# Splitting float32 weights in the DMA instead of on VectorE and GpSimd, in a two-layer encoder trunk

## The chip, the cores and the metric

The kernel runs on one core of a Trainium2 chip. The metric is the device time of one execution in microseconds; lower is better. TensorE (PE in the profile) multiplies, VectorE (DVE), ScalarE (ACT) and GpSimd (POOL) work on tiles in the on-chip memory, SyncE (SP) issues DMAs. Every engine takes its own instructions in a fixed order, and waits where an operand or a buffer is not ready.

## What is computed

```python
for l in range(DEPTH):                                                  # 2 layers
    x = x + 0.5 * swiglu(rms_norm(x, ffn1_norm[l]), ffn1_w_in[l], ffn1_w_out[l])
    x = x + hybrid_mixer(rms_norm(x, mix_norm[l]), mix_w_in[l], ...)    # conv | stick-breaking | retention
    x = x + 0.5 * swiglu(rms_norm(x, ffn2_norm[l]), ffn2_w_in[l], ffn2_w_out[l])
return rms_norm(x, final_norm)

def swiglu(h, w_in, w_out):
    gate, up = jnp.split(h @ w_in, 2, axis=-1)
    return (jax.nn.silu(gate) * up) @ w_out
```

x has 512 rows of 1024 float32 numbers. The hidden size of the half steps is 2816, 22 blocks of 128. The mixer projects to 24 blocks of 128 columns, runs a causal convolution of 31 taps on 256 channels, eight heads of stick-breaking attention and four of retention, and projects back.

## The kernel before

x lies transposed: eight tiles of 128 features by 512 tokens. All products use float32r operands, each float32 operand being split into two of them, a high part `hi` (the number rounded to float32r) and a low part `lo` (the rest). A product of a weight block with a block of x takes three matmuls of 512 columns: `hi` by x's high part, `hi` by x's low part, `lo` by x's high part (`product`). Each of them streams 512 columns.

A weight unit is what one accumulator needs: 128 output features by up to eight blocks of 128 input features, [128, 8, 128] float32, 512 KB, each partition's share being contiguous in HBM. Units are

- `f1_in`, `f2_in`: 44 a half step (gate and up for each of 22 blocks), eight blocks each, accumulators `pg` and `pu` (`pf` for the first two);
- `f1_out`, `f2_out`: eight output tiles for each of three parts of the hidden size, of 8, 8 and 6 blocks, accumulator `po`;
- `m_in`: 24 a mixer, accumulators `pf` (the first four, in `conv_in`) and `pj`;
- `m_out`: eight output tiles in two halves of four blocks, accumulator `mo` (`out_first`, `out_last`).

For each unit `load` issues a DMA from SP into `w_raw`; `split_unit` then lets ScalarE cast it into `w_hi` (`split_of`), and VectorE subtract to get `w_lo`. In the middle of the mixer (`weight`, called by `project` and `out_first`) GpSimd subtracts. The two units at the very start are loaded and split in halves of four blocks, with the cast on VectorE. The pool `w` has three buffers each of `w_raw`, `w_hi` and `w_lo`.

The half step (`ffn`) runs over the 22 blocks in three parts; within a part first gate and up for each block, with `g`, `s`, `u` (scale, silu, product) and the split of the result into `hh` and `hl`, then the eight output tiles, each added to x through `t`: on GpSimd in the first two parts, on VectorE in the last. The norm's sum of squares uses ScalarE (`sq`) and GpSimd, its inverse root is a power on GpSimd (`rt`), and its spread over the partitions a matmul (`bc`, copied to `rstd`).

The mixer is made of threads whose instructions are interleaved when the program is built, by `weave`, after estimates in `Times`: an instruction of GpSimd is booked as 0.13 us plus 0.00286 us an element of a partition, a DMA of SP as 2.5 us. VectorE takes the taps of the convolution's first half (`yc`), ScalarE and GpSimd most of those of the second.

The order on every engine and queue is fixed before the run by the framework's scheduler, from its own estimate of when each operand and buffer is ready; it need not be the order of the program's lines. Semaphores are placed by it too. Every recorded instruction goes through `TimedEngine.run`, so the profile gives line 92 for all.

Of the kernel before, what the change touches and what calls it, by code (L numbers as in the profile page):

```python
# [4 lines left out]
F32 = mybir.dt.float32  # L5
# [6 lines left out]
P = 128  # L12
# [15 lines left out]

# of the mixer's order of work, in us: the slack before a product's operands are taken to be there, the time from one
# engine to another, how far behind the tensor engine the others may be, and the time between taps of the convolution  # L30
MARGIN, SIGNAL, BEHIND, PACE = 0.6, 0.2, 4.0, 2.3
# engine -> (time of an instruction, time per element)
COST = {"vector": (0.08, 0.00137), "scalar": (0.16, 0.00101), "gpsimd": (0.13, 0.00286)}
STEP = 4  # parts of a product between which other work may come
SHARED_TAPS = 24  # taps that ScalarE and GpSimd take for the second half of the channels


class Times:
    """Estimates, in us, of when instructions end, for the order in which to give them out."""

# [29 lines left out]
class Timed:  # L70
    """The machine, with a note of each instruction's times."""

# [24 lines left out]
class Kernel:  # L97
    def __init__(self, tc, io, out):
        self.tc, self.nc, self.io, self.out = tc, Timed(tc.nc), io, out

# [1 line left out]
    def split_of(self, src, hi, lo, engine=None, early=False):  # L102
# [6 lines left out]

    def load(self, src, n, step=KT):  # L110
        raw = self.wpool.tile([P, KT, P], F32, name="w_raw", tag="w_raw")
        for k in range(0, n, step):
            e = min(k + step, n)
            self.nc.sync.dma_start(raw[:, k:e, :], src[:, k:e, :])
        return raw

    def split_unit(self, raw, n, engine=None, step=KT):
        hi = self.wpool.tile([P, KT, P], F32R, name="w_hi", tag="w_hi")
        lo = self.wpool.tile([P, KT, P], F32R, name="w_lo", tag="w_lo")
        for k in range(0, n, step):  # L120
            e = min(k + step, n)
            self.split_of(raw[:, k:e, :], hi[:, k:e, :], lo[:, k:e, :], engine, step < KT)
        return hi, lo

    def unit(self, src, n, engine=None):
        return self.split_unit(self.load(src, n), n, engine)

    def product(self, acc, w, rhs_hi, rhs_lo, order, first=True, last=True):
        """acc[M, S] (+)= sum over order's (k of w, k of rhs) of w_k.T @ rhs_k, both operands in two parts."""
        hi, lo = w  # L130
        mm = self.nc.tensor.matmul
        for i, (a, b) in enumerate(order):
            mm(acc, hi[:, a, :], rhs_hi[b], start=first and i == 0, stop=False)
            mm(acc, hi[:, a, :], rhs_lo[b], start=False, stop=False)
            mm(acc, lo[:, a, :], rhs_hi[b], start=False, stop=last and i == len(order) - 1)
# [4 lines left out]
    def products(self, units, rhs_hi, rhs_lo):  # L140
        """Products of several weight units with rhs, whose parts get ready one by one."""
        accs = [self.bank("pf") for _ in units]
        for k in range(KT):
            for acc, w in zip(accs, units):
                self.product(acc, w, rhs_hi, rhs_lo, [(k, k)], k == 0, k == KT - 1)
        return accs

# [1 line left out]
    def new_norm(self):  # L149
        self.acc = []  # L150

    def norm_add(self, d, last=False, engine=None):
        """Adds x[d]'s squares to the running sum over d."""
        nc = self.nc
        sq = self.small.tile([P, S], F32, name="sq", tag="sq" if d else "sq_acc")
        nc.scalar.activation(sq, self.x[d], ACT.Square)
        if d and not (last and d == KT - 1):
            (engine or nc.gpsimd).tensor_tensor(out=self.acc[0], in0=self.acc[0], in1=sq, op=ALU.add)
        else:
            self.acc.append(sq)  # L160
# [11 lines left out]
    def diagonals(self, r):  # L172
        """[token, TT] -> [P, S], each token's value on the diagonal of its tile."""
        dg = self.small.tile([P, TT, P], F32, name="dg", tag="dg")
# [22 lines left out]
    def x_ready(self, d, g, engine=None):  # L197
        """x[d] has its value for the next norm, with gain g."""
        nc = self.nc
# [6 lines left out]

# [1 line left out]
    def ffn(self, w_in, w_out, after, first=None):  # L208
# [48 lines left out]

# [1 line left out]
    # Its parts are threads that give out their instructions piece by piece. A piece ends with a yield of the tiles that  # L259
    # the next one's matrix products read, of a time to let pass, or of a condition to wait for.  # L260
    def weave(self, threads):
# [17 lines left out]
    def weight(self, unit, n=KT):  # L279
        return self.unit(unit, n, self.nc.gpsimd)  # L280

    def project(self, unit):
        """A generator: the product's bank."""
        ps = self.bank("pj")
# [31 lines left out]
    def twice(self, q):  # L316
        """[2 * 64, S] of two heads -> high and low parts [P, head, S], each head's rows in both halves."""
        nc = self.nc
# [9 lines left out]
    def stacked(self, k):  # L328
        """[2 * 64, S] of two heads -> [P, head, S], a head's high part in its own rows and its low part in the others."""
        t = self.mq.tile([P, 2, S], F32R, name="kk")  # L330
# [5 lines left out]
    def values(self, unit, centred):  # L336
        """v of a pair of heads, [token, TT, part, feature]; parts: high and low of head 0, low and high of head 1.

        Centred over each head's features, so that the weighted sums are too.
        """  # L340
        nc = self.nc
# [21 lines left out]

    # key tile -> (bank, first column); a key tile's queries are those from it on
    BANKS = ((S, ((1, 0), (3, 3 * P))), (2 * P, ((2, 0),)), (S, ((0, 0),)))
    WHERE = {0: (2, 0), 1: (0, 0), 2: (1, 0), 3: (0, 3 * P)}

    def scores(self, q, k, e, masked):
        """Key-major scores of head e of a pair, by bank."""
        mm = self.nc.tensor.matmul  # L370
# [22 lines left out]
    def weighted(self, wts, vv, e, out):  # L393
        """out = sum over keys of the weights times v, [64 features, S]."""
        nc = self.nc
        y = self.att.tile([P, S], F32, name="y", tag="y", bufs=1)
        # the first one covers the bank
        passes = [(0, 0), *((kt, i) for kt in (1, 3, 2) for i in range(2)), (0, 1)]
# [12 lines left out]
    def exp_ln(self, out, src, f, **kw):  # L411
        """An exp or ln, kept behind the load of the tables that have both."""
        i = self.nc.scalar.activation(out, src, f, **kw)
        self.after_on_act(i, self.tables)
        self.exps.append(i)
# [85 lines left out]

    # the parts of y in the order in which the outward projection's halves take them: convolution 0, 1; sticks 2 to 5;
    # retention 6, 7
    HALVES = ((2, 6, 3, 4), (7, 0, 1, 5))

    def split_y(self, m, y):
        """A generator: y, part m, split, when its place is free."""
        h = int(m in self.HALVES[1])
# [7 lines left out]

    # pairs of heads in their order: (retention?, number in its kind)
    PAIRS = ((False, 0), (True, 0), (False, 1), (False, 2), (True, 1), (False, 3))

    def attention(self, gain):  # L520
        """All heads in turn."""
        for i, (ret, p) in enumerate(self.PAIRS):
# [42 lines left out]
    def inputs(self, w_in):  # L565
        """All projections of heads, in the order in which they are needed."""
        for i, (ret, p) in enumerate(self.PAIRS):
            # the buffers are those of two pairs before
            yield lambda i=i: self.scored >= 2 * i - 2
# [85 lines left out]
    def out_first(self, w_out):  # L655
        """The first half of the outward projection."""
        yield lambda: all(m in self.y_done for m in self.HALVES[0])
# [43 lines left out]
    def run(self):  # L701
        tc, nc, io = self.tc, self.nc, self.io
        with (
            tc.tile_pool(name="const", bufs=1) as cp,
            tc.tile_pool(name="state", bufs=1) as st,
            tc.tile_pool(name="small", bufs=1) as self.small,
            tc.tile_pool(name="w", bufs=3) as self.wpool,
            tc.tile_pool(name="mm", bufs=4, space=PSUM) as self.mm,
# [7 lines left out]
            nc.sync.dma_start(self.x[0], io["x"][:, 0, :])  # L716
            first = [self.load(io["f1_in"][0][0, i], KT, STEP) for i in range(2)]
            for d in range(1, KT):
# [20 lines left out]
            for d in range(KT):  # L739
                self.x_ready(d, g[0], nc.vector)  # L740
                if d < 2:
                    first[d] = self.split_unit(first[d], KT, step=STEP)

# [125 lines left out]
```

## Time and profile before

| | |
|---|---|
| time, median of 3 runs | 2085.26 us (2083.88, 2085.26, 2087.13) |
| span of the profiled execution | 2083.2 us |
| what the median has beyond that span | 2.1 us |
| TensorE matmuls | 8826, busy 1998.4 us (96%) |
| VectorE busy | 1144.5 us (55%) |
| ScalarE busy | 764.0 us (37%) |
| GpSimd busy | 377.8 us (18%) |
| DMA | 187.95 MB, mean 90 GB/s |
| HBM read | 176.00 MB |
| mean granted clock of TensorE | 0.982 |

No time of its own is given for the profiled execution; its span runs from the first to the last instruction, and the runs' times lie 0.7 to 3.9 us above it. Matmuls overlap each other, so their busy time is more than the time they add; the chain that ended last shows their true pace. A group's row gives the line, the engine, the operation, output and inputs with shapes and the count, then busy time and the mean of one in ns, then the engine's idle time just before and who ended it. A row of a timeline gives start and length in us. In the windows each stretch has its length and then the busy time of PE, PEld (weight load of TensorE), DVE, ACT and POOL, the granted clock, the share of the 16 DMA engines and GB/s.

### The profile page before, as it was taken

How to read it: one execution, taken by the hardware profiler on the slowest of the kernel's cores; microseconds unless marked ns; L12 is line 12 of the kernel's file. 1: busy time of each engine (PE TensorE's matmuls, PEld its weight loads, DVE VectorE, ACT ScalarE, POOL GpSimd, SP SyncE). 2: the span in 40 equal slices, each digit the busy share in tenths (PEclk: the TensorE clock that was granted, in tenths of full speed). 3: DMA queues.
4: the chain of work that ended last, by engine and by line, in shares of the span. 5: the costliest groups of instructions: out<-in, count | busy, mean ns of one | idle time of the engine just before them, and what ended most of it. 6: DMA issues, size and time to landing. Idle time of an engine off the chain costs nothing.

```text
span 2083.2 us, 22414 instructions
## 1 busy us (share of the span) xinstructions
PE 1998.4 (96%) x8826; PEld 1624.5 (78%) x8826; DVE 1144.5 (55%) x1338; ACT 764.0 (37%) x1103; POOL 377.8 (18%) x240
## 2 busy tenths in 40 slices
PE   8999999968999999999999999999689999999997
PEld 6888888857778888888888888887577878888885
DVE  5444444687877444444634535457878664544534
ACT  4212223446756322222422222243557552222222
POOL 0020000455232001010100101015553220100102
PEclk9999999989999999999999999999899999999998
DMA  5232332322212333232323233232221132233321
GB/s 199 91 101 91 91 101 81 104 63 69 70 47 94 101 91 101 91 96 92 98 94 97 92 99 94 90 99 85 71 71 51 60 113 91 91 101 91 97 83 63
DMA packets 60778, 187.95 MB, mean 90 GB/s; under 512 B 8320, under 2 KB 8832, under 8 KB 60544
## 3 DMA queue, kind: packets, MB, share of 16 engines
q1 hardware_dynamic: 60672, 186.52, 28.7%
q8 instruction: 69, 1.13, 0.2%
q14 instruction: 37, 0.30, 0.0%
HBM read 176.00 MB, written 2.10 MB: 85 GB/s over the span
## 4 chain that ended last, share of the span: by engine, by line
PE 85%; DVE 8%; ACT 2%; issue 2%; POOL 1%; DMA 0%; DVEq 0%; SPq 0%; ACTq 0%; POOLq 0%
PE po L92 23%; PE pg L92 23%; PE pu L92 23%; PE pf L92 4%; PE pj L92 4%; DVE yc L92 3%; PE mo L92 3%; PE z L92 3%; DVE ll L92 1%; PE y L92 1%; ACT sp L92 1%; POOL w_lo L92 1%; POOL yc L92 0%; ACT w_hi L92 0%; DVE w_lo L92 0%
## 5 line engine op out<-in xcount | busy, mean ns | idle before, releaser
L92 ACT CAST w_hi<-w_raw 128x1024 fp32r<-128x1024 f32 (+2 forms) x350 | 346.2, 991 | 1066.2 <-PE pg L92 326.9
L92 DVE TENSOR_TENSOR w_lo<-w_raw,w_hi 128x1024 fp32r<-128x1024 f32 (+2 forms) x298 | 414.2, 1391 | 43.0 <-ACT w_hi L92 28.3
L92 PE MATMUL po<-hh,w_hi 128*128 128x512 f32 x704 | 274.4, 390 | 0.0
L92 PE MATMUL po<-hh,w_lo 128*128 128x512 f32 x704 | 274.3, 390 | 0.0
L92 PE MATMUL po<-hl,w_hi 128*128 128x512 f32 x704 | 274.2, 389 | 0.0
L92 PE MATMUL pu<-xh,w_hi 128*128 128x512 f32 x672 | 267.3, 398 | 0.0
L92 PE MATMUL pg<-xh,w_hi 128*128 128x512 f32 x672 | 266.0, 396 | 0.0
L92 PE MATMUL pg<-xh,w_lo 128*128 128x512 f32 x672 | 265.8, 396 | 0.0
L92 PE MATMUL pu<-xl,w_hi 128*128 128x512 f32 x672 | 265.7, 395 | 0.0
L92 PE MATMUL pu<-xh,w_lo 128*128 128x512 f32 x672 | 265.7, 395 | 0.0
L92 PE MATMUL pg<-xl,w_hi 128*128 128x512 f32 x672 | 265.6, 395 | 0.0
L92 POOL TENSOR_TENSOR x<-x,t 128x512 f32<-128x512 f32 x64 | 87.7, 1370 | 934.8 <-DVE t L92 914.0
L92 DVE TENSOR_TENSOR u<-pu,s 128x512 f32<-128x512 f32 x84 | 58.1, 691 | 291.4 <-PE pu L92 291.4
L92 DVE TENSOR_TENSOR g<-pg,rstd 128x512 f32<-128x512 f32 x84 | 58.0, 691 | 229.4 <-PE pg L92 229.4
L92 DVE SCALAR_TENSOR_TENSOR t<-po,rstd 128x512 f32<-128x512 f32 x96 | 66.4, 692 | 187.1 <-PE po L92 187.1
L92 POOL TENSOR_TENSOR w_lo<-w_raw,w_hi 128x1024 fp32r<-128x1024 f32 (+1 forms) x56 | 122.2, 2183 | 180.0 <-ACT w_hi L92 180.0
L92 PEld LDWEIGHTS po<-hh,w_lo 128*128 128x128 f32 x704 | 132.2, 188 | 27.6
L92 PEld LDWEIGHTS po<-hl,w_hi 128*128 128x128 f32 x704 | 132.3, 188 | 27.5
L92 PEld LDWEIGHTS po<-hh,w_hi 128*128 128x128 f32 x704 | 132.2, 188 | 27.4
L92 PEld LDWEIGHTS pu<-xl,w_hi 128*128 128x128 f32 x672 | 126.2, 188 | 31.4 <-issue 1.0
L92 PEld LDWEIGHTS pu<-xh,w_hi 128*128 128x128 f32 x672 | 126.2, 188 | 31.4 <-issue 1.0
L92 PEld LDWEIGHTS pu<-xh,w_lo 128*128 128x128 f32 x672 | 126.2, 188 | 30.6
(143 smaller groups left out, 3053.9 us busy)
## 6 DMA issues: line engine op xcount, KB each, us to landing
w_raw<-in_f_in SPq DMA_DIRECT2D x174, 512.0 KB, 3.3
w_raw<-in_f_out SPq DMA_DIRECT2D x64, 512.0 KB, 3.5
w_raw<-in_m_in SPq DMA_DIRECT2D x48, 512.0 KB, 3.3
w_raw<-in_f_out SPq DMA_DIRECT2D x32, 384.0 KB, 3.1
w_raw<-in_m_out SPq DMA_DIRECT2D x32, 256.0 KB, 2.8
qh<-qh SPq DMA_DIRECT2D x24, 128.0 KB, 2.2
ql<-ql SPq DMA_DIRECT2D x24, 128.0 KB, 2.2
x<-in_x SPq DMA_DIRECT2D x8, 256.0 KB, 6.3
```

What stands on the lines that cost most here:

```text
L92: return f(*args, **kw)
```

## The change

`load`, `split_unit` and `w_raw` go. `unit` takes each weight twice from HBM, both times with a DMA issued by GpSimd: the first converts float32 to float32r on the way into `w_hi`; ScalarE then writes the negative of `w_hi` into `w_lo`; the second DMA adds the float32 weights to `w_lo`. VectorE and GpSimd subtract no weights any more. The pool `w` has four buffers each of `w_hi` and `w_lo`. The first two units are still taken in halves, which are now converted and negated like all others. `split_of` remains for the other operands. Comments are removed.

```diff
-    def load(self, src, n, step=KT):
-        raw = self.wpool.tile([P, KT, P], F32, name="w_raw", tag="w_raw")
-        for k in range(0, n, step):
-            e = min(k + step, n)
-            self.nc.sync.dma_start(raw[:, k:e, :], src[:, k:e, :])
-        return raw
-
-    def split_unit(self, raw, n, engine=None, step=KT):
+    def unit(self, src, n, step=KT):
+        nc = self.nc
         hi = self.wpool.tile([P, KT, P], F32R, name="w_hi", tag="w_hi")
         lo = self.wpool.tile([P, KT, P], F32R, name="w_lo", tag="w_lo")
         for k in range(0, n, step):
             e = min(k + step, n)
-            self.split_of(raw[:, k:e, :], hi[:, k:e, :], lo[:, k:e, :], engine, step < KT)
+            nc.gpsimd.dma_start(hi[:, k:e, :], src[:, k:e, :])
+            nc.scalar.activation(lo[:, k:e, :], hi[:, k:e, :].bitcast(F32), ACT.Copy, scale=-1.0)
+            nc.gpsimd.dma_start(lo[:, k:e, :], src[:, k:e, :], accum_op=ALU.add)
         return hi, lo
 
-    def unit(self, src, n, engine=None):
-        return self.split_unit(self.load(src, n), n, engine)
-
...
     def weight(self, unit, n=KT):
-        return self.unit(unit, n, self.nc.gpsimd)
+        return self.unit(unit, n)
...
-            tc.tile_pool(name="w", bufs=3) as self.wpool,
+            tc.tile_pool(name="w", bufs=4) as self.wpool,
...
-            first = [self.load(io["f1_in"][0][0, i], KT, STEP) for i in range(2)]
+            first = [self.unit(io["f1_in"][0][0, i], KT, STEP) for i in range(2)]
...
                 self.x_ready(d, g[0], nc.vector)
-                if d < 2:
-                    first[d] = self.split_unit(first[d], KT, step=STEP)
```

## The prediction

> **What bounds the kernel now.** First the totals and the slices of the page, then the chain that ended last, then the stretches.
>
> ```profile
> span 2083.2 us, 22414 instructions
> PE 1998.4 (96%) x8826; PEld 1624.5 (78%) x8826; DVE 1144.5 (55%) x1338; ACT 764.0 (37%) x1103; POOL 377.8 (18%) x240
> DMA  5232332322212333232323233232221132233321
> PE 85%; DVE 8%; ACT 2%; issue 2%; POOL 1%; DMA 0%; DVEq 0%; SPq 0%; ACTq 0%; POOLq 0%
> ```
>
> TensorE makes 85% of the chain, DMA 0%: weights arrive early enough. From the chain in order of time (start, length, what) and the windows (length; busy time of PE, PEld, DVE, ACT, POOL; clock; DMA share; GB/s):
>
> ```profile
> 102.19 43.55 PE po L92 x192
> 145.73 5.60 PE pg L92 x24
> 346.10 32.68 PE po L92 x144
> 616.30 2.79 PE mo L92 x12
> ...
> 10.00:15.00 5.00, 5.00 (x15) 3.65 (x15) 4.74 (x8) 5.00 (x10) 0.00 (x0) 1.00 1.05 406
> 235.00:279.00 44.00, 44.00 (x196) 36.41 (x195) 23.71 (x18) 9.31 (x10) 9.03 (x7) 1.00 0.30 93
> 404.00:470.00 66.00, 48.72 (x201) 38.91 (x200) 58.68 (x56) 29.29 (x45) 37.20 (x19) 0.84 0.22 68
> 470.00:640.00 170.00, 156.08 (x784) 129.85 (x783) 132.46 (x194) 108.82 (x198) 64.83 (x38) 0.98 0.22 64
> ```
>
> In the half steps TensorE never rests. One weight unit lasts 24 matmuls: 5.60 us inward, 43.55 / 8 = 5.44 outward, 32.68 / 8 = 4.09 for six blocks; 2.79 for four in the mixer's outward projection. So a faster split gains nothing there, and a unit that comes more slowly than one per 5.6 us costs at once. Only the mixer has slack: 66.0 - 48.7 + 170.0 - 156.1 = 31 us of idle TensorE a layer.
>
> **The change part by part.** Removed are the loads on SP and these groups:
>
> ```profile
> L92 ACT CAST w_hi<-w_raw 128x1024 fp32r<-128x1024 f32 (+2 forms) x350 | 346.2, 991 | 1066.2 <-PE pg L92 326.9
> L92 DVE TENSOR_TENSOR w_lo<-w_raw,w_hi 128x1024 fp32r<-128x1024 f32 (+2 forms) x298 | 414.2, 1391 | 43.0 <-ACT w_hi L92 28.3
> L92 POOL TENSOR_TENSOR w_lo<-w_raw,w_hi 128x1024 fp32r<-128x1024 f32 (+1 forms) x56 | 122.2, 2183 | 180.0 <-ACT w_hi L92 180.0
> ...
> w_raw<-in_f_in SPq DMA_DIRECT2D x174, 512.0 KB, 3.3
> w_raw<-in_f_out SPq DMA_DIRECT2D x64, 512.0 KB, 3.5
> w_raw<-in_f_out SPq DMA_DIRECT2D x32, 384.0 KB, 3.1
> w_raw<-in_m_in SPq DMA_DIRECT2D x48, 512.0 KB, 3.3
> w_raw<-in_m_out SPq DMA_DIRECT2D x32, 256.0 KB, 2.8
> ```
>
> With two more units that load in halves: 176 inward, 64 + 32 outward, 48 + 32 in the mixers. *Subtractions:* 414 us leave VectorE and 122 GpSimd, all beside other work in the half steps. In the mixer VectorE is 58.7 / 66 = 89% busy, and its convolution taps stand on the chain:
>
> ```profile
> L92 DVE SCALAR_TENSOR_TENSOR yc<-cv,p_conv_w,yc 128x512 f32<-128x512 f32 x74 | 92.1, 1245 | 1.8
> L92 DVE SCALAR_TENSOR_TENSOR t<-po,rstd 128x512 f32<-128x512 f32 x96 | 66.4, 692 | 187.1 <-PE po L92 187.1
> ```
>
> A tap reads two tiles and takes 1.245 us, while an instruction of the same kind off PSUM takes 0.692; if GpSimd's subtractions are what stretches it, up to 37 x 0.55 = 20 us a layer come back, and at most the 31 us idle. Against that GpSimd's taps, squares and powers now queue behind DMAs that wait. I take 10 us a layer, -20; bounds -62 and +60 (the same idle doubled).
>
> *Negation:* it replaces the cast on ScalarE.
>
> ```profile
> L92 ACT CAST w_hi<-w_raw 128x1024 fp32r<-128x1024 f32 x286 | 299.8, 1050 | 970.0 <-PE pg L92 311.0 <-PE po L92 283.3 <-issue 273.4
> L92 ACT ACTIVATE xh<-x,gains 128x512 fp32r<-128x512 f32 x48 | 34.2, 719 | 38.1 <-DVE x L92 31.8 <-DMA x<-in_x 6.3
> L92 ACT CAST hh<-u 128x512 fp32r<-128x512 f32 x88 | 54.7, 621 | 2.4 <-DVE u L92 1.4
> ```
>
> Scaled copies cost 0.72 - 0.62 = 0.10 more than casts: 1.05 + 0.10 = 1.15 us a unit (bounds 1.05 and 2 x 0.72 = 1.44). 350 x 0.1 = 35 us more on an engine 37% busy: nothing by itself. Behind a negation that waits for its DMA stand the silu and the cast of hh; I cost that at nothing, because ScalarE idled 1066 us ahead of these same instructions.
>
> *Traffic:* every unit is read twice, and the addition reads the negated half as well. A plain unit costs the 16 engines 0.30 x 5.6 = 1.7 us (1.3 at the 406 GB/s of the fifth of the windows). For the addition the bounds are 1.3 (only the 512 KB written count) and 6.8 (its two streams of 1.7 at half speed); I take both streams, 3.4. Together 5.1 of 5.6 us, 91%: it still fits, barely.
>
> The Trainium skill, Collectives: The Full Stack, "The bandwidth ceiling: the fold count and why AG ≠ RS ≠ AR", says that the adder in a DMA engine is free but its two source reads go down one ring, halving the rate. By it the addition is 2 x 1.7 = 3.4 us and the slow-path rival falls; were it 1.7, the best order would load the engines 61%. No row before holds an adding DMA.
>
> *Order:* this is the step that decides. Both transfers go through GpSimd's queue, the second waits for the negation, which waits for the first. Behind that wait stand the next unit's first transfer and GpSimd's own work:
>
> ```profile
> L92 POOL TENSOR_TENSOR x<-x,t 128x512 f32<-128x512 f32 x64 | 87.7, 1370 | 934.8 <-DVE t L92 914.0
> L92 POOL TENSOR_TENSOR rt<-ms,mhalf 128x4 f32<-128x4 f32 (+1 forms) x13 | 20.3, 1565 | 82.0 <-DVE ms L92 82.0
> ...
> L92 SPq DMA_DIRECT2D w_raw<-in_f_in x178: 327/328/432, 1.6 to 1999.3; - x178
> DMA to landing us min/median/max: 2.6/3.3/6.6
> ...
> 156.78 1.05 ACT L92 CAST w_hi<-w_raw 128x1024 fp32r<-128x1024 f32 x1 [4.05 <-PE pu L92]
> 157.77 0.63 ACT L92 CAST hh<-u 128x512 fp32r<-128x512 f32 x1
> 162.38 1.05 ACT L92 CAST w_hi<-w_raw 128x1024 fp32r<-128x1024 f32 x1 [3.99 <-PE pg L92]
> 163.33 0.62 ACT L92 ACTIVATE s<-g 128x512 f32<-128x512 f32 x1
> 163.46 1.22 DVE L92 TENSOR_TENSOR w_lo<-w_raw,w_hi 128x1024 fp32r<-128x1024 f32 x1 [0.20 <-ACT w_hi L92]
> ```
>
> The ScalarE rows show that the order on an engine is not the program's: casts of later units, freed by the end of a product, stand ahead of hh and s. So a first transfer stands where its buffer was expected free, every 5.6 us, and a second where its negation was expected done. GpSimd's issue isn't shown: bounds 0.33 (SP's) and 1.57 (GpSimd's smallest operation), I take 1.0, between. Alone, first transfer to second takes 1.0 + 3.3 + 1.15 + two hops of about 0.18 = 5.8 us against 5.6: both orders will occur. With 1.6 us of landing beside the 1.7 of data, one queue in order, and 1.5 for negation and hops:
> - each second transfer ahead of the next unit's first: 1.0 + 1.6 + 3.4 + 1.7 + 1.5 = 9.2 us a unit;
> - two firsts, then two seconds: (1.0 + 1.6 + 6.8 + 1.7 + 1.5) / 2 = 6.3;
> - a first always ahead: 5.1, hidden under 5.6.
>
> I take the middle, 6.3, for the mixture. Scaled to six blocks it is 5.1, to four 3.95. Sum: 176 x 0.7 = 123; 64 x 0.86 = 55; 32 x 1.0 = 32; the mixers' first four units 8 x 0.7 = 6; their last eight 16 x 1.16 = 19. The middle of a mixer needs 20 x 6.3 + 8 x 3.95 = 158 us in 236: hidden.
>
> The Trainium skill, DMA: Bandwidth & Descriptors, "Latency and other measured facts", gives GpSimd's DMAs a first byte at about 1 us, SP's 0.6: an estimate of 0.2 us more a unit in pairs, some 60 us in all. No row here shows it.
>
> *Start:* chain, and who waits:
>
> ```profile
> 2.11 4.65 DMA w_raw<-in_f_in
> 7.21 1.20 DVE w_lo L92 x2
> ```
>
> The first low part is ready at 8.4; after it must come a negation (0.7) and a second transfer (3.3 and its issue) instead of casts and subtraction (1.2): +5, bounds 2 and 10. *Norms:* seven powers on GpSimd may stand behind a waiting transfer, 0 to 5.8 us each; I take 2, +14. *Four buffers for three, no raw tile:* lead grows by one unit; nothing at a steady rate.
>
> Sum: 123 + 55 + 32 + 6 + 19 - 20 + 5 + 14 = +234 on 2083.2: 2317. The median of the runs is 2085.3, 2.1 above the span: 2319.
>
> **Rivals.**
> 1. *Hidden, and faster:* first transfers always ahead, the unit's two transfers under 5.6 us. For it: the engines are 70% idle now. Then the mixers' gain shows: up to 31 idle, or what the taps lose, about 20, with some 5 of chain for other subtractions: -50, +5, +7: 2083 - 38 + 2 = 2047. It decides at 5.6 us a unit: an addition up to 3.9 us still fits, in that order alone.
> 2. *Strict alternation*, 9.2 us: 176 x 3.6 + 64 x 3.76 + 32 x 3.6 + 8 x 3.6 + 16 x 3.4 - 1 = +1072: 3157. For it: the order is fixed before the run, and 5.8 lies close to 5.6. Against: one late estimate breaks the alternation.
> 3. *Slow data path* in converting or adding transfers: 3.4 + 6.8 = 10.2 us: 176 x 4.6 + 64 x 4.76 + 32 x 3.6 + 8 x 4.6 + 16 x 2.3 = +1303, with 37 for start, norms and the mixers' middle, 20 x 10.2 + 8 x 5.1 in 236: 3425. Nothing in the trace speaks for or against.
>
> **How the numbers follow.** Mixed order 0.44 (2100 to 2700; 2319), alternation 0.18, slow path 0.12, hidden 0.26, of which faster 0.16, same 0.04, slower 0.06. The bound of 0.2% is about what three runs spreading 0.16% can tell. Slower: 0.44 + 0.18 + 0.12 + 0.06 = 0.80. Range 2040 to 3100: out are the slow path and a few hundredths at either side.
>
> **What would show it.** Right: gaps between units in pg, pu and po with the low part's DMA as their releaser; the DMA share near 0.8; GpSimd's transfers waiting on ScalarE, and the next firsts right behind; VectorE near 730 us, ScalarE near 800; taps nearer 0.7 than 1.25 us. Wrong: products still at 5.60 us (hidden); a DMA share near 1 with long landings (slow path); landing to landing of about 9 us at a share near 0.55 (alternation). If GpSimd's issue is several us, it, not order or data, sets the pace.

## The result and the profile after

| | before | after |
|---|---|---|
| time, median of 4 runs each | 2084.57 us (2082.25 to 2087.13) | 2385.99 us (2380.70 to 2394.78) |
| ratio, 95% interval | | 1.1455 [1.1428, 1.1483] |
| span of the profiled execution | 2083.2 us | 2378.8 us |

The changed kernel is slower by 14.6%; 2319 us with a range of 2040 to 3100 was predicted. Its page, in totals, slices, HBM and the shares of the chain:

```profile
span 2378.8 us, 22577 instructions
PE 2103.0 (88%) x8826; PEld 1659.3 (70%) x8826; DVE 693.9 (29%) x1036; ACT 756.8 (32%) x1107; POOL 737.7 (31%) x892
DMA  8767776765546777776767676667654467776674
HBM read 347.97 MB, written 2.10 MB: 147 GB/s over the span
issue 26%; PE 25%; DMA 24%; POOL 10%; ACT 6%; DVE 3%; SPq 0%; POOLq 0%; DVEq 0%; ACTq 0%
```

TensorE's share of the chain fell from 85% to 25%. What stands there instead is the circle of first transfer, negation and second transfer, in which each waits for the one before. Who waited (engine and tile, released by: total us, times, longest):

```profile
POOL w_lo L92 <- ACT w_lo L92: 1305.6, 306, 9.0
DVE hl L92 <- ACT hh L92: 372.8, 86, 8.5
PE po L92 <- DMA w_lo<-in_f_out: 51.0, 32, 3.3
PE pu L92 <- DMA w_lo<-in_f_in: 37.9, 21, 3.6
PE pg L92 <- DMA w_lo<-in_f_in: 35.4, 24, 2.9
PE po L92 <- ACT hh L92: 24.6, 9, 6.5
```

GpSimd stood 1305.6 us, over half of the span, in front of second transfers whose negation was not done. TensorE itself waited for low parts in these rows 77 times, 124 us together, never longer than 3.6. How one such wait comes about is in GpSimd's timeline (start, length, what, in brackets the idle time before it and its releaser):

```profile
163.18 0.87 POOL L92 DMA_DIRECT2D w_lo<-in_f_in  x1 [0.42 <-ACT w_lo L92]
163.72 0.88 POOL L92 DMA_DIRECT2D w_hi<-in_f_in  x1
164.29 1.60 POOL L92 TENSOR_TENSOR x<-x,t 128x512 f32<-128x512 f32 x1
172.65 0.86 POOL L92 DMA_DIRECT2D w_lo<-in_f_in  x1 [6.76 <-ACT w_lo L92]
173.28 1.56 POOL L92 TENSOR_TENSOR x<-x,t 128x512 f32<-128x512 f32 x1
174.53 1.38 POOL L92 DMA_DIRECT2D w_hi<-in_f_in  x2
181.10 0.88 POOL L92 DMA_DIRECT2D w_lo<-in_f_in  x1 [5.20 <-ACT w_lo L92]
182.57 0.87 POOL L92 DMA_DIRECT2D w_lo<-in_f_in  x1 [0.59 <-ACT w_lo L92]
183.12 0.89 POOL L92 DMA_DIRECT2D w_hi<-in_f_in  x1
```

The `w_hi` at 163.72 goes out at once behind the `w_lo` before it, although its buffer may have been free for long; then no transfer can leave the queue until its negation is done, at 172.65. The next `w_hi` stand behind that, two of them in the row at 174.53. One first and one second, from 163.72 to 174.53, take 10.8 us; two firsts and two seconds, from there to 183.12, take 8.6 us for both. That is three units in 19.4 us, 6.5 us a unit, where TensorE uses one up in 5.6. The turns with a single first are the costly ones; the pair runs at 4.3 us a unit. The chain through the same place (start, length, what):

```profile
165.90 6.74 issue
...
175.90 5.18 issue
...
181.10 5.46 DMA w_lo<-in_f_in
...
186.61 6.96 PE pu L92 x22
```

"issue" of 5 to 7 us is the time in which a first transfer lands and is negated; among the DMA issues of the page the row for the inward `w_hi` gives a landing of 6.4 us (median), so little else fits in.

Where the 295.6 us of the span went is read from the times at which each norm's `rstd` is copied. The differences between one and the next, in us (HS: half step, M: mixer):

| | start | HS1 | M1 | HS2 | HS1, layer 2 | M2 | HS2, layer 2 |
|---|---|---|---|---|---|---|---|
| before | 29.4 | 367.9 | 290.8 | 367.9 | 367.9 | 289.9 | 359.2 |
| after | 41.3 | 423.9 | 309.4 | 433.7 | 434.6 | 310.7 | 414.6 |
| five `w_hi` (below) | 41.3 | 368.3 | 287.0 | 368.7 | 369.7 | 289.2 | 355.0 |

The four half steps lose 243.9 us, the mixers 39.4, the start 11.9 (the rest is rounding and the end, behind the last norm). The border between the start and the first half step needs care, because one product changed sides. On the chain before, the norm's spread (`bc`) stands ahead of the product `pu`:

```profile
28.52 0.86 PE bc L92 x2
29.38 5.60 PE pu L92 x24
```

With the change it stands behind it (these lines are of the kernel with five buffers, whose first norm is at 41.3 us too):

```profile
34.82 5.60 PE pu L92 x24
40.42 0.87 PE bc L92 x2
```

So 5.6 of the 11.9 us are work of the half step that is now done before the norm. Like for like the start loses 6.3 us and the half steps 249.5.

In the windows (length; PE, PEld, DVE, ACT, POOL; clock; DMA share; GB/s) the second half step, from norm to norm, and two short stretches of the first are, after,

```profile
774.60:1208.30 433.70, 389.75 (x1595) 306.74 (x1595) 75.18 (x111) 102.55 (x130) 127.32 (x159) 0.96 0.70 160
186.60:190.60 4.00, 3.99 (x11) 3.20 (x12) 0.00 (x0) 0.21 (x1) 0.00 (x0) 0.57 0.82 222
190.60:193.60 3.00, 3.00 (x14) 2.44 (x13) 0.00 (x0) 1.37 (x2) 1.42 (x2) 1.00 0.05 7
```

and the second half step before is

```profile
688.20:1056.20 368.00, 368.00 (x1596) 298.73 (x1596) 169.97 (x180) 104.77 (x130) 32.70 (x24) 1.00 0.30 95
```

Of the 65.7 us more, 433.7 - 389.75 = 44 are idle time and 22 are TensorE being busy for longer at the same work (1595 matmuls against 1596). The granted clock accounts for most of these 22: 0.96 over 433.7 us is 17 us of full clock lost. The two short stretches show where it goes: behind the wait that ends at 186.61 the granted clock is 0.57 for four microseconds, then 1.00.

### The profile page after: what moved, and what is told of

It is laid out like the page before. It is cut to its first block, busy times and chain, and to the rows that moved or that the text cites. A ratio compares the mean times of both kernels' runs of the same rounds, so it can differ in the third digit from the quotient of the medians.

```text
span 2378.8 us, 22577 instructions
## 1 busy us (share of the span) xinstructions
PE 2103.0 (88%) x8826; PEld 1659.3 (70%) x8826; DVE 693.9 (29%) x1036; ACT 756.8 (32%) x1107; POOL 737.7 (31%) x892
## 3 DMA queue, kind: packets, MB, share of 16 engines
q8 instruction: 70, 1.15, 0.2%
## 4 chain that ended last, share of the span: by engine, by line
issue 26%; PE 25%; DMA 24%; POOL 10%; ACT 6%; DVE 3%; SPq 0%; POOLq 0%; DVEq 0%; ACTq 0%
DMA w_hi<-in_f_in 6%; DMA w_lo<-in_f_in 6%; PE pu L92 6%; PE pg L92 5%; PE po L92 5%; DMA w_hi<-in_f_out 5%; ACT w_lo L92 4%; POOL w_hi L92 3%; PE pf L92 3%; DMA w_hi<-in_m_in 3%; POOL w_lo L92 3%; PE pj L92 2%; POOL x L92 2%; PE z L92 1%; PE mo L92 1%
## 5 line engine op out<-in xcount | busy, mean ns | idle before, releaser
L92 ACT ACTIVATE w_lo<-w_hi 128x1024 fp32r<-128x1024 f32 (+2 forms) x354 | 351.6, 994 | 1410.7 <-issue 558.3
L92 POOL DMA_DIRECT2D w_lo<-in_f_in x178 | 155.1, 871 | 749.8 <-ACT w_lo L92 719.3
L92 PE MATMUL po<-hh,w_lo 128*128 128x512 f32 x704 | 288.9, 410 | 51.0 <-DMA w_lo<-in_f_out 51.0
L92 PE MATMUL pu<-xh,w_lo 128*128 128x512 f32 x672 | 275.0, 409 | 37.9 <-DMA w_lo<-in_f_in 37.9
L92 PE MATMUL po<-hh,w_hi 128*128 128x512 f32 x704 | 286.4, 407 | 24.6 <-ACT hh L92 24.6
L92 PE MATMUL po<-hl,w_hi 128*128 128x512 f32 x704 | 286.2, 407 | 1.1 <-DVE hl L92 1.1
L92 POOL DMA_DIRECT2D w_lo<-in_f_out x96 | 84.3, 878 | 405.2 <-ACT w_lo L92 405.2
L92 PEld LDWEIGHTS pg<-xh,w_lo 128*128 128x128 f32 x672 | 127.5, 190 | 77.4 <-DMA w_lo<-in_f_in 47.5
L92 DVE TENSOR_TENSOR hl<-u,hh 128x512 fp32r<-128x512 f32 x88 | 60.9, 693 | 372.9 <-ACT hh L92 372.8
L92 PEld LDWEIGHTS po<-hl,w_hi 128*128 128x128 f32 x704 | 138.3, 196 | 35.1 <-DVE hl L92 4.9
L92 PEld LDWEIGHTS pg<-xh,w_hi 128*128 128x128 f32 x672 | 128.0, 191 | 38.2 <-DVE xl L92 3.7
```

The costliest lines, as they stand in the source:

```text
L92: return f(*args, **kw)
```

## The experiments

The theory: the time is set by the order in GpSimd's queue. Rivals: the data path (an addition that costs too much), ScalarE or GpSimd as engines, and the number of buffers. Each edit is against the changed kernel. "Ahead" counts, in the program's fixed order on GpSimd (not a row of the profile), in how many of 273 steps from unit to unit in the half steps the next first transfer stands ahead of the second: 100 in the changed kernel.

**Every first transfer behind the second before it** (ahead: 0 of 273). The edge orders, without a semaphore.

```diff
-            nc.gpsimd.dma_start(hi[:, k:e, :], src[:, k:e, :])
+            i = nc.gpsimd.dma_start(hi[:, k:e, :], src[:, k:e, :])
+            if self.second is not None:
+                self.behind(i, self.second)          # order only
...
-            nc.gpsimd.dma_start(lo[:, k:e, :], src[:, k:e, :], accum_op=ALU.add)
+            self.second = nc.gpsimd.dma_start(lo[:, k:e, :], src[:, k:e, :], accum_op=ALU.add)
```

> The changed kernel with one rule more: each unit's first transfer is placed behind the second transfer of the unit before it, so the queue alternates strictly. Theory (the order in GpSimd's queue sets the pace): the stretch in the changed kernel's trace where a second transfer stands ahead of the next unit's first takes 9.5 us from one second transfer to the next, so every unit takes about 9.5 us: 3200 to 3300 us in all. Rival (the amount of data, or the time of the DMA engines, sets the pace, whatever the order): 2386 us, within 50.

Measured: 2930.93 us, 1.4075 [1.4046, 1.4104]. The direction holds, the size was overstated. GpSimd's timeline, with ScalarE's negation before the last row:

```profile
322.39 0.87 POOL L92 DMA_DIRECT2D w_lo<-in_f_in  x1 [7.46 <-issue]
322.94 0.89 POOL L92 DMA_DIRECT2D w_hi<-in_f_in  x1
...
329.17 1.06 ACT L92 ACTIVATE w_lo<-w_hi 128x1024 fp32r<-128x1024 f32 x1 [3.44 <-DMA w_hi<-in_f_in]
330.53 0.86 POOL L92 DMA_DIRECT2D w_lo<-in_f_in  x1 [6.70 <-ACT w_lo L92]
```

This turn is 330.53 - 322.39 = 8.14 us: 0.55 to the next issue, 6.23 until the first has landed and its negation begins, 1.06 for the negation, 0.30 to the next issue. The prediction had 9.2. The mean is a little longer than the turn shown: from 200 to 400 us the kernel moves 126 GB/s, which is 8.3 us for the 1.05 MB of a unit's two transfers.

**Every second transfer behind the next unit's first**, in the half steps alone, the units being planned one ahead (ahead: 270 of 273; four buffers as in the changed kernel).

```diff
+        i = nc.gpsimd.dma_start(lo[:, :n, :], src[:, :n, :], accum_op=ALU.add)
+        if then:                                     # the next unit, its first transfer is out
+            self.behind(i, then[4])
```

> In the half steps each unit's second transfer is placed behind the next unit's first, so one first transfer is always ahead; buffers and transfers as in the changed kernel, mixers unchanged. Theory (order): the half steps go back to 5.6 us a unit and lose the 244 us that they gained, about 2140 us (2100 to 2200). Rival (amount of data): 2386, within 30. A middle value means that the data path binds next.

Measured: 2167.53 us, 1.0406 [1.0386, 1.0425]. As expected: the half steps take 373.2, 377.5, 375.7 and 354.5 us, 18 more than before in all, in place of 244. Of the other 65 us the mixers have 51 (314.2 and 317.2) and the start 14; their order this edit leaves as it was.

**The second transfer without its addition**, a plain copy over the negated half. It leaves the subtraction out, so the low part is not the right one; the order stays (100 ahead).

```diff
-            nc.gpsimd.dma_start(lo[:, k:e, :], src[:, k:e, :], accum_op=ALU.add)
+            nc.gpsimd.dma_start(lo[:, k:e, :], src[:, k:e, :])
```

> The second transfer converts the weights into the low part's buffer instead of adding them to it; so nothing is subtracted and the low part is wrong, all else is as in the changed kernel, order too. Theory (order, with the adding transfer's second stream in the cycle): the cycle of three units, 19.8 us, loses three times some 1.5 us and falls under the 16.8 us of TensorE: 2100 to 2200 us. Rival (waiting for issue, landing and negation, not data): 2330 to 2400 us.

Measured: 2115.34 us, 1.0158 [1.0138, 1.0179], as its theory expected: in the very order of the changed kernel 271 of the 301 us are back, and the half steps take 370.7, 372.4, 374.3 and 357.8. First transfers land after 4.7 us (median, inward units) in place of 6.4, second ones after 4.0 in place of 5.5. So the loss needs both: the order, which makes TensorE wait for the round trip, and the addition, which makes the round trip long enough to be felt.

The windows of this kernel and of the one with five `w_hi`, where TensorE is never idle either:

```profile
150.00:350.00 200.00, 200.00 (x864) 161.75 (x864) 33.81 (x49) 52.25 (x63) 49.57 (x81) 1.00 0.61 186
```

```profile
150.00:350.00 200.00, 200.00 (x865) 161.78 (x864) 33.89 (x49) 51.56 (x63) 62.49 (x83) 1.00 0.90 186
```

At equal GB/s of HBM, a unit per 5.6 us keeps the DMA engines busy for 0.61 x 5.6 = 3.4 us with two plain transfers, 1.7 each, and for 0.90 x 5.6 = 5.0 with the addition, which therefore costs 3.3, twice the plain one. The Trainium skill, Collectives: The Full Stack, "The bandwidth ceiling: the fold count and why AG ≠ RS ≠ AR", counts two source reads for an adding transfer; by that rule it takes 3.4, and this pair of windows agrees. The pair also shows that 5.0 us of DMA a unit does not slow a product down while a first transfer is always ahead. What the DMA engines can carry bounds nothing here; what the addition costs is time in the round trip.

**High part from a raw tile by SP and a cast on ScalarE**, so that GpSimd issues the adding transfer alone (three buffers each).

```diff
+        raw = self.wpool.tile([P, KT, P], F32, name="w_raw", tag="w_raw", bufs=3)
...
-            nc.gpsimd.dma_start(hi[:, k:e, :], src[:, k:e, :])
+            nc.sync.dma_start(raw[:, k:e, :], src[:, k:e, :])
+            nc.scalar.copy(hi[:, k:e, :], raw[:, k:e, :])
```

> The first transfer goes back to SP (a plain load into a raw tile, cast by ScalarE into the high part); negation and the adding transfer of GpSimd stay. Three buffers each for raw, high and low part. Theory (the first transfers stand behind the second ones in GpSimd's one queue): without them there GpSimd's queue holds only adding transfers, the half steps run at 5.6 us a unit, 2080 to 2120 us, although the bytes read are the same. Rival (the chain of load, negation and addition is too long for the buffers whatever the queue): 2200 us or more.

Measured: 2139.64 us, 1.0263 [1.0237, 1.0289], 20 us above what was expected. The steady part came out (half steps 372 to 378, the last 359.8; mixers 291.8 and 294.0): with the two transfers in two queues the half steps lose 22 us in all in place of 244, and the mixers 5 in place of 39. The miss is the start, 55.6 us to the first norm against 29.4 (most of a product stands ahead of it here too). On its chain stand two adding transfers of 11 us to landing:

```profile
10.82 11.17 DMA w_lo<-in_f_in
...
35.45 11.05 DMA w_lo<-in_f_in
```

**Negation on VectorE.**

```diff
-            nc.scalar.activation(lo[:, k:e, :], hi[:, k:e, :].bitcast(F32), ACT.Copy, scale=-1.0)
+            nc.vector.tensor_scalar(out=lo[:, k:e, :], in0=hi[:, k:e, :].bitcast(F32), scalar1=-1.0, scalar2=None, op0=ALU.mult)
```

> The negation goes to VectorE, which is idle 71% of the time; else the changed kernel. The shorter negation shifts the order that is fixed for GpSimd's queue: 200 of 273 second transfers of the half steps now stand ahead of the next unit's first, 173 in the changed kernel. Theory (order): slower though the negation is quicker, 2400 to 2530 us. Rival (ScalarE's own queue, where silu and casts stand behind negations that wait for a DMA): faster, 2300 to 2370 us.

Measured: 2540.26 us, 1.2191 [1.2167, 1.2215]: 10 above the expected bound, right in direction. The negation itself became shorter, by the groups of this kernel and of the changed one:

```profile
L92 DVE TENSOR_SCALAR w_lo<-w_hi 128x1024 fp32r<-128x1024 f32 (+2 forms) x354 | 248.6, 704 | 1377.0 <-DMA w_hi<-in_f_in 837.2 <-DMA w_hi<-in_f_out 453.0 <-DMA w_hi<-in_m_in 52.7
```

```profile
L92 ACT ACTIVATE w_lo<-w_hi 128x1024 fp32r<-128x1024 f32 (+2 forms) x354 | 351.6, 994 | 1410.7 <-issue 558.3
```

A negation 0.29 us faster, on an engine that is otherwise less busy, made the kernel 154 us slower. The first transfers, taken all together, land after 6.1 us (median) in both kernels, so they aren't what became longer. What also changed is the order: 73 ahead instead of 100. So the shorter negation did not pay for the order that came with it. How much of the 154 is the order and how much is work on VectorE that now stands behind a negation, this run does not tell.

**Converting transfer alone**: `w_hi` by the converting DMA, raw tile by SP, subtraction on VectorE and, in the mixers, GpSimd, as before; no addition.

```diff
+            nc.sync.dma_start(raw[:, k:e, :], src[:, k:e, :])
             nc.gpsimd.dma_start(hi[:, k:e, :], src[:, k:e, :])
-            nc.scalar.activation(lo[:, k:e, :], hi[:, k:e, :].bitcast(F32), ACT.Copy, scale=-1.0)
-            nc.gpsimd.dma_start(lo[:, k:e, :], src[:, k:e, :], accum_op=ALU.add)
+            (engine or nc.vector).tensor_tensor(out=lo[:, k:e, :], in0=raw[:, k:e, :], in1=hi[:, k:e, :].bitcast(F32), op=ALU.subtract)
```

> Only the converting transfer of the change: GpSimd's DMA writes the high part, SP loads the raw tile too, VectorE and (in the middle of the mixers) GpSimd subtract as before; three buffers each. Theory: GpSimd's queue holds only first transfers that wait for nothing but a buffer, so nothing is lost, 2075 to 2105 us. Rival (converting transfers are slow, or GpSimd's DMAs land late): 2150 us or more.

Measured: 2147.84 us, 1.0310 [1.0293, 1.0327]; a miss, 43 above the expected bound. In the half steps conversion costs little (371.8, 375.3, 375.4 and 357.8, 17 us in all). The loss is 17 us in each mixer (308.1, 306.4) and 13 at the start (42.4). That in the mixers GpSimd's subtractions and the transfers hold each other up in one queue is the likely reason; it was not tried.

**A fifth buffer for the high part** (ahead: 272 of 273, and all 80 in the mixers).

```diff
-        hi = self.wpool.tile([P, KT, P], F32R, name="w_hi", tag="w_hi")
+        hi = self.wpool.tile([P, KT, P], F32R, name="w_hi", tag="w_hi", bufs=5)
```

> The changed kernel with five buffers for the high part instead of four (low part four). The order fixed for GpSimd's queue then has the next unit's first transfer ahead of each second one. Theory (order): like the run with one first transfer always ahead, in the mixers' dense stretches too: 2080 to 2150 us. Rival (amount of data): 2386, within 30, since a buffer more adds lead and no pace.

Measured: 2093.85 us, 1.0054 [1.0039, 1.0069]. As expected, with 4 KB a partition 292 of 301 us are back. GpSimd's timeline now has one first and one second per product:

```profile
250.90 0.85 POOL L92 DMA_DIRECT2D w_lo<-in_f_out  x1
254.29 0.55 POOL L92 DMA_DIRECT2D w_hi<-in_f_out  x1 [2.55 <-PE po L92]
255.09 1.29 POOL L92 TENSOR_TENSOR x<-x,t 128x512 f32<-128x512 f32 x1 [0.25 <-DVE t L92]
256.34 0.84 POOL L92 DMA_DIRECT2D w_lo<-in_f_out  x1
259.73 0.55 POOL L92 DMA_DIRECT2D w_hi<-in_f_out  x1 [2.55 <-PE po L92]
```

The first waits for TensorE to free its buffer, and the second behind it for nothing. Both intervals are 5.44 us, TensorE's own pace.

**Five buffers, strict alternation** (ahead: 0 of 273): the edits of the first experiment and of the one above together. It tells the buffers from the order that they brought.

> Five buffers for the high part, as in the run at 2094 us, but each first transfer placed behind the second transfer of the unit before, as in the run at 2931 us. Theory (order, not buffers): about 2930 us, within 40. Rival (the fifth buffer's lead): under 2400 us.

Measured: 2935.93 us, 1.4092 [1.4067, 1.4117], no better than 2930.93 with four. While the order alternates, the fifth buffer is worth nothing; it acts through the order that the scheduler gives out.

**The 64 additions to x on VectorE instead of GpSimd.**

```diff
-                        nc.gpsimd.tensor_tensor(out=self.x[d], in0=self.x[d], in1=t, op=ALU.add)
+                        nc.vector.tensor_tensor(out=self.x[d], in0=self.x[d], in1=t, op=ALU.add)
```

> The changed kernel with the 64 additions of the half steps' results to x on VectorE instead of GpSimd; the order of the transfers stays the same (173 of 273 second transfers ahead of the next first). Theory (the transfers' own order sets the pace): within 40 us of the changed kernel, 2345 to 2390 us, the gain being the additions' own 1.6 us where they stand before a transfer. Rival (GpSimd's other work in the same queue is a large part of the loss): under 2300 us.

Measured: 2388.00 us, 1.1461 [1.1437, 1.1486]: no gain, and still 100 ahead. These additions aren't what holds the transfers up.

**Five buffers, and the first two units by SP, with cast and subtraction as before.** This and the next two pursue the half per cent that five buffers still lack.

```diff
-            first = [self.unit(io["f1_in"][0][0, i], KT, STEP) for i in range(2)]
+            # raw tiles by nc.sync.dma_start in halves; later, for d < 2:
+                        self.split_of(raw[:, k:e, :], hi[:, k:e, :], lo[:, k:e, :], None, True)
```

> The changed kernel with five buffers for the high part (order with the next first transfer ahead, 2094 us) and the first two units of the program loaded by SP and split on VectorE as before. Theory (what is left over the kernel before is its late start, 41.3 us instead of 29.4 to the first norm): 12 us less, 2078 to 2086 us, no slower than the kernel before. Rival (what is left is spread, by DMA traffic): 2088 to 2095 us.

Measured: 2090.51 us, 1.0041 [1.0025, 1.0057], with the first norm at 37.4 instead of 41.3 us; a miss for the theory, and the rival's range holds. The time of the first norm is a poor measure here, since nearly all of a product stands ahead of it in these kernels and behind it before; the next whole product (`pg`) starts at 38.81 us, with five buffers alone at 42.67, before at 34.98. So about half of the late start was removed. On the chain stands SP's load itself, now 8.34 us to landing where the chain of before had 4.65; GpSimd's first transfers of later units run beside it.

**The same, GpSimd's transfers held back until SP's loads have landed**, by order behind a small copy that reads the last of them.

```diff
+            self.hold = nc.gpsimd.tensor_copy(held, raw[:, KT - 1, 0:1])
...
+            if self.hold is not None:
+                self.behind(i, self.hold)            # each first transfer
```

> Five buffers and the first two units from SP (2090.5 us, first norm at 37.4 us), and GpSimd's first three transfers held until SP's loads of those two units have landed. Theory (at the start they take DMA time from SP's loads, whose landing took 8.3 us instead of 4.7): first norm at 30 to 33 us, 2082 to 2087 us, the kernel before within 0.3%. Rival (the late start is the negation and addition chain of the third unit): 2088 to 2092 us.

Measured: 2089.51 us, 1.0028 [1.0018, 1.0039]; the first norm came at 37.1, not 30 to 33, a miss again, and the rival's range holds. SP's loads did land sooner, after 4.9 us (median) in place of 6.6, but the next product starts at 38.45, hardly earlier. The chain gives the next thing that is late, the third unit's adding transfer:

```profile
16.61 8.10 DMA w_lo<-in_f_in
```

**The same with four units by SP.**

```diff
+            for i in range(2):                       # units 3 and 4: raw by nc.sync, then
+                self.split_of(raw, hi, lo)
```

> Five buffers, the first four units of the program from SP and split as before, GpSimd's first transfers held until SP's loads have landed. Theory (the late start is the chain of first transfer, negation and addition of the third unit, 24.7 us at its end): first norm at 29 to 31 us, 2080 to 2084 us, level with the kernel before or just under it. Rival (some of the rest is spread over the half steps): 2085 to 2090 us.

Measured: 2083.96 us beside 2082.89 for the kernel before, 1.0005 [0.9993, 1.0016]: level. With GpSimd held, SP's first load lands after 5.16 us on the chain, and each stage is within 6 us of that of before. The first norm is at 35.1, not 29 to 31; but that is the product ahead of it: the next one starts at 36.45, 1.5 us later than before. No version was faster than the kernel before.

## Why the prediction was right

*The deciding step holds.* The prediction said that the order in GpSimd's one queue decides, that it would be mixed, and that a mixture gives 6.3 us a unit. Order alone moves the time from 2931 through 2386 to 2168 with four buffers (0, 100 and 270 ahead) and from 2936 to 2094 with five. The pace in the quoted stretch is 6.5, and over the second half step 1.05 MB a unit at 160 GB/s give 6.6. The range of 2040 to 3100 proves little by itself: the strict alternation, at 2931, lies in it as well.

*Right in size, in part by luck.* The 6.3 was worked out for two firsts, then two seconds. Such a pair takes 8.6 us in the quoted stretch and 9.5 (median) over all inward units of the trace, 4.3 to 4.7 a unit: it would be hidden. The single turn, which the prediction priced at 9.2 for alternation, takes 10.8 in the stretch and 9.3 (median) in the trace, and it makes the loss. That one of each, (9.3 + 9.5) / 3, comes out at 6.3 a unit again is luck.

The half steps and the norms were put at 210 + 14 = 224, that is 56 each; with the product that changed sides they lost 61.5, 65.8, 66.7 and 55.5. But the 56 were all to be gaps. In the second half step 44 us are; of the other 22 some 17 are the lower clock, which the sum does not have. Nor are all gaps from low parts: "I cost that at nothing", it said of `hh` behind a waiting negation, and TensorE waited 24.6 us for `hh`, which the waits of before and of five buffers do not list; VectorE's wait for it went from 2.7 us before to 71.7 with five buffers and 372.8 after.

*The mixers failed.* +25 less 20 were predicted, 39.4 measured. Two terms were wrong:
- "The middle of a mixer [...] hidden": it was set against a time that all units share evenly. With the order mended by the fifth buffer the mixers take 287.0 and 289.2, so all of the 39.4 is the order again, and in the middle too: there TensorE waited 12.2 us for low parts of `pj`, a wait that no row has with five buffers.
- The 20 us of relief. The taps did get shorter when GpSimd's subtractions went, from 1245 to 913 ns in the changed kernel, to 934 with five buffers:

```profile
L92 DVE SCALAR_TENSOR_TENSOR yc<-cv,p_conv_w,yc 128x512 f32<-128x512 f32 x74 | 69.1, 934 | 1.7
```

Yet with five buffers the mixers gain only 3.8 and 0.7 us. VectorE's taps weren't what the mixer waits for alone. Among the chain's pieces in the first mixer there now stand transfers like

```profile
459.53 6.35 DMA sw<-q
```

which are small transfers between on-chip tiles that SP issues for the rotation of `q`. Landing took them 2.0 us (median) before and takes 4.1 here. Twice the weight traffic cannot be the whole reason, since in the changed kernel, which reads twice too, they land after 2.0. That these eat the relief is an inference; it was not tried alone. Another candidate, also untried, is the order of the mixer's own instructions: `weave` books the transfers of the weights otherwise now, and TensorE's rows in the mixer stand in another order than before.

*The start:* +5 predicted, with bounds of 2 and 10; 6.3 measured, like for like (11.9 by the norm). The size held, though not its main term: the adding transfer was taken at 3.3 us to landing, as SP's loads; at the start it lands after 8 to 11, as three experiments' chains show.

*Sizes.* GpSimd's issue was taken as 1.0 us: from one to the next it is 0.55. Data of 1.7 and 3.4 us: 1.7 and 3.3 measured. Negation 1.15: 1.06. DMA share "near 0.8": 0.70 in the second half step. VectorE "near 730" and ScalarE "near 800": 694 and 757. Alternation at 9.2: 8.14 in the turn shown, of which issue is 0.55 for 1.0, landing and data 6.23 for 6.7, negation and hops 1.36 for 1.5; 3157 was 2931.

*The rivals.* "Hidden, and faster" is what the queue does with one first always ahead, the hidden part at least: TensorE never rests between 150 and 350 us. The faster part failed with the mixers' relief; 2047 became 2094. The slow data path fell as a bound: at a share of 0.90 products run at full pace. But the addition's time matters in the mixed order, as the run without it shows (2115 for 2386).

## What to carry to other kernels

Where two dependent transfers of a unit share one in-order queue, look at the order before the bytes: with a first transfer always ahead the round trip cost nothing here, in strict alternation the full round trip was paid for every unit, and one more buffer of the first operand can decide which order a scheduler gives out. In a mixed order a shorter round trip helps as well: without the addition nine tenths of the loss were gone. A chain of work moved to DMA can pay only where the engine it relieves was the bound; here TensorE was, and the best version came out level with the kernel before. Price an adding transfer as two plain ones on the DMA engines, and where nothing can run ahead of it, by its measured time to landing.

## What was not expected of the hardware

The clock. After waits of TensorE as short as 2 to 3 us matmuls can run at nearly half pace. The changed kernel's timeline behind one of them:

```profile
186.61 0.80 PE L92 MATMUL pu<-xh,w_lo 128*128 128x512 f32 x1 [2.29 <-DMA w_lo<-in_f_in]
187.20 0.63 PE L92 MATMUL pu<-xh,w_hi 128*128 128x512 f32 x1
187.63 0.63 PE L92 MATMUL pu<-xl,w_hi 128*128 128x512 f32 x1
```

They start 0.43 us apart where TensorE's own pace is 0.233, and 22 of them last 6.96 us instead of 22 x 0.233 = 5.1: this wait costs 1.8 us more than its length. The Trainium skill, TensorE: Matmul & The Clock Gate, "Part 1: The HAM clock gate (the "warmup" mystery)", describes half speed after at least one idle window of about 3.4 us and a return to full speed after about 3.4 us of sustained work. The return agrees: the rows are slow for a good 3 us. The idle time does not, since the row shows 2.29. Nor does the length alone decide: behind a wait of 2.90 us that ends at 167.26 the granted clock is 1.00 from 167.2 to 171.2. By the trace's clock records a stretch at half rate begins during, or within 3.4 us after, 19 of the 28 waits of 2 to 3 us. No experiment isolated it, but a queue that feeds TensorE late pays it with many of its gaps.

Also new: an instruction on VectorE that reads two on-chip tiles, the tap `yc`, went from 1245 to 913 ns (mean) when GpSimd's subtractions went. The kernel with the converting transfer alone, in which GpSimd still subtracts, is the control: 1187 ns.
